# One pair of v columns computed plainly, with the mLSTM's gate columns in the same pass

## The chip, the cores and the metric

The kernel runs on one core of a Trainium2 chip. The core's engines run on their own instruction streams and meet through semaphores: TensorE (PE in the profile; PEld is its loading of the stationary operand), VectorE (DVE), ScalarE (ACT), GpSimd (POOL), and SyncE (SP), which issues nearly all DMAs. The metric is the device time of one execution in microseconds (us).

## The reference

One layer of an encoder on 1024 prompt and 256 sample tokens of width 2048, all float32. What matters here is its beginning, the normalization and the one combined projection, whose columns feed all later parts:

```python
hn = rmsnorm(x, norm_w)
proj = jnp.einsum('btd,dp->btp', hn, w_in)
cuts = [int(c) for c in np.cumsum([NA_WIDTH] * 4 + [2 * ML_WIDTH, ML_WIDTH, ML_WIDTH, ML_WIDTH])]
na_q, na_k, na_v, na_g, ml_qk, ml_v, ml_o, ml_z, ml_gp = jnp.split(proj, cuts, axis=-1)
...
gates = ml_gp.astype(f32).reshape(B, T, 2, 2, ML_HEADS) + gate_b.astype(f32)
h = bidirectional_mlstm(mq, mk, mv, gates)
```

The projection has 9 x 1024 columns and 16 gate columns. Queries, keys and values of the neighbourhood attention (8 heads of 128) come first, then its SiLU gate, then the mLSTM's q and k (which pass a convolution of width 5), v, o and z. The factors norm_w (by K) and 1/rms (by token) can be taken apart: the kernel multiplies x by norm_w beforehand, and the result of a projection by the token's 1/rms afterwards.

## The kernel before

**Number format.** Each float32 operand is split into a high and a low part that TensorE takes (hi is a rounded copy, made on ACT; lo = source - hi, made on DVE; functions split and split_a). A product is three matmuls: hi x hi, hi x lo, lo x hi.

**Stages.** The first stage (up to about 1095 us) projects the first 768 tokens; the second stage projects the other 512 tokens, and attention, mLSTM and the output projection follow and interleave. This change is in the first stage.

**A pair of the first stage** (pair_a). The 72 tiles of 128 columns are taken in pairs, named by the first tile's number: 0 to 7 q, 8 to 15 k, 16 to 23 the gate of the attention, 24 to 39 q and k of the mLSTM, 40 to 47 o, 48 to 55 z, 56 to 71 the values (256 columns a pair). A pair is a 2 x 2 x 2 block product (two column tiles, two halves of K = 2048, two halves of 384 tokens), done with seven products instead of eight, in the manner of Strassen and Winograd. The seven combinations of x are made once and stay in SBUF (xop(i, kk, b_) gives combination i, K tile kk, hi or lo). 1 is the first half of K of the first tokens and 2 the second half of K of the same tokens; 3 is the second half of K of the other tokens, and 7 that minus their first half of K. The combinations of weights are sums of 256 columns on POOL (summed, tiles named t), split into tiles named s. The weights are the stationary operand and 384 tokens the moving one: 7 products x 8 K tiles x 3 = 168 matmuls of 384 columns a pair. The seven PSUM banks are then added up on DVE (plus) and scaled by 1/rms (scaled), which gives the two tiles c with columns on the partitions and tokens along the free axis.

**What follows a pair** (finish_a) is a generator that the next pair drives on between its own products: splits and stores for q and k, the convolution for 24 to 38 (many DVE operations), tanh on ACT and a store for o and z. Values are wanted with tokens on the partitions, so a pair of v needs 12 transposes on PE (L475), after which they are copied as hi and lo into a tile vo and stored (store_v).

**The gates** (gates_a) run once, behind pair 6: weight sums on DVE, four tiles that POOL clears and that take the split weights, 64 matmuls of 384 tokens (L596), two copies, and six small products (L604) that bring the tokens to the partitions; DVE then scales by 1/rms and adds the bias into gt.

**The order of the pairs** is a list:

```python
order = [4, 6]
rest = list(range(KT0, QK0, 2)) + list(range(OT0, NCH, 2))
for i in range(NU):
    order += [QK0 + 2 * i, NCH + 2 * i, *rest[2 * i : 2 * i + 2]]
```

It gives 4, 6, 24, 56, 8, 10, 26, 58, 12, 14, ... (KT0 = 8, QK0 = 24, OT0 = 40, NCH = 56). Before some pairs, x_square loads a tile xq of the other tokens and squares it on ACT. Ten of the pairs (SECOND: 24, 8, 10 among them) also store four of their weight sums (sD) for the second stage.

**Buffers.** Weight tiles of 512 KB (named r) and the tiles xq share a ring of three (tag ra); splits of weights a ring of eight (wsa); results and what is made from them a ring of five (pc); vo has one buffer besides. PSUM has three banks under the tag pr and five under a. Who comes when on each engine, and which free buffer a tile gets, is settled by a scheduler with a model of its own when the program is built; the code's order gives the priorities.

**In the second stage** proj_v does what its name says with the tokens as the stationary operand and the weights as the moving one. Its first call takes the 16 gate columns along as columns 257 to 272 (tile pv, L774).

Of the kernel before, what the change touches and what calls it, by code (L numbers as in the profile page):

```python
# [14 lines left out]
P = 128  # L15
# [33 lines left out]
def kernel(  # L49
# [3 lines left out]
    xtok: bass.AP,  # L53
    w_in: bass.AP,
    w_g: bass.AP,
    w_o: bass.AP,
    lnw: bass.AP,
    rpb_tab: bass.AP,
# [14 lines left out]
    def f(ap):  # L73
        return ap.bitcast(F32)

    def bank(tag, name):
        return ps.tile([P, 512], F32, tag=tag, name=name, bufs=3 if tag == "pr" else 5)
# [106 lines left out]
    def split_a(hi, lo, src):  # L184
        S.copy(hi, src)  # L185
        last_split["ins"] = V.tensor_tensor(lo, src, f(hi), op=ALU.subtract).ins
# [102 lines left out]
    def pc(name):  # L289
        return wa.tile([P, GA], F32, tag="pc", name=name, bufs=NPC)  # L290

    def wsa(name):
        return wa.tile([P, 2, 256], F32R, tag="wsa", name=name, bufs=NWS)
# [145 lines left out]
    def finish_a(n1, Cn):  # L439
# [28 lines left out]
        if n1 >= NCH:  # L468
# [3 lines left out]
            for tt in range(GA // P):  # L472
# [8 lines left out]
                store_v((n1 - NCH) // 2, tt * P, vo, b[:, :256])  # L481
                yield

    def pair_a(n1, bg=iter(()), hook=None, first=False, pinned=False):
        nm = f"A{n1}"
        tags = ("pr", "pr", "pr", "a", "a", "a", "a")
# [82 lines left out]
            pass  # L569
        return finish_a(n1, Cn)  # L570

    def gates_a():
        raw = wa.tile([P, 1024], F32, tag="ra", name="gAw", bufs=NRA)
        DM.dma_start(raw[:, :256], w_g)
        ab = [raw[:, :P], raw[:, P : 2 * P]]
        ext = [raw[:, 256 : 256 + P], raw[:, 384 : 384 + P]]
        V.tensor_tensor(ext[0], ab[0], ab[1], op=ALU.add)
        V.tensor_scalar(ext[1], ab[0], -1.0, None, op0=ALU.mult)
        st = []
        for i, src in enumerate((*ab, *ext)):  # L580
            t = wsa(f"gAt{i}").rearrange("p h c -> p (h c)")[:, : 8 * 32 + 96]
            G.memset(f(t), 0.0)
            tv = t[:, :256].rearrange("p (k h c) -> p k h c", h=2, c=16)
            sv = src.rearrange("p (k c) -> p k c", c=16)
            split_a(tv[:, :, 0, :], tv[:, :, 1, :], sv)
            st.append(t)
        sel = raw[0:32, 512:528]
        V.tensor_tensor(sel, ident[0:32, 0:16], ident[0:32, 16:32], op=ALU.add)
        gs = pc("gAg")
        for th, prods in enumerate((((0, 1), (1, 2)), ((2, 3), (3, 7)))):  # L590
            b = bank("a", f"gAb{th}")[:, :HALF]
            n = 0
            for w_, i in prods:
                for kk in range(8):
                    for hl_ in range(2):
                        PE.matmul(  # L596
                            b, st[w_][:, kk * 32 : kk * 32 + P], xop(i, kk, hl_),
                            start=n == 0, stop=n == 31,
                        )
                        n += 1  # L600
            V.tensor_copy(gs[0:32, th * HALF : (th + 1) * HALF], b[0:32])
        for tt in range(GA // P):
            b = bank("a", f"gAt{tt}")
            PE.matmul(b[:, :16], gs[0:32, tt * P : (tt + 1) * P], sel, start=True, stop=True)  # L604
            V.scalar_tensor_tensor(
                gt[:, tt, :], b[:, :16], rcs[0][:, tt : tt + 1], gb_sb, op0=ALU.mult, op1=ALU.add
            )

    opening = first_tiles()
    next(opening)  # L610
    cw_sb = const.tile([P, 16, 5], F32, tag="cw", name="cw_sb")
# [6 lines left out]
    DM.dma_start(w4_sb, mlnw)  # L618
    V.tensor_scalar(w4_sb, w4_sb, 0.25, None, op0=ALU.mult)
    order = [4, 6]  # L620
    rest = list(range(KT0, QK0, 2)) + list(range(OT0, NCH, 2))
    for i in range(NU):
        order += [QK0 + 2 * i, NCH + 2 * i, *rest[2 * i : 2 * i + 2]]
    pools = []

    def second_pools():
# [3 lines left out]

    bg = opening
    for i, n1 in enumerate(order):
        bg = pair_a(n1, bg, second_pools if i == len(order) - 1 else None, i == 0, i == 1)
        if i == 1:
            gates_a()
        k = i - 4
        if 0 <= k < 8:
            x_square(1, k)
        if k == 8:
            x_rstd(1)  # L640
# [1135 lines left out]
def _layout(inputs):  # L1776
    import numpy as np

    g = {k: np.asarray(v) for k, v in inputs.items()}
    x = np.concatenate([g["x_prompt"][0], g["x_sample"][0]], axis=0)  # L1780
    xT = np.ascontiguousarray(x.reshape(TT, KT, P).transpose(2, 1, 0))
    w = g["w_in"][0]
    cols = {}
    o = 0
    for name, n in (("q", 1024), ("k", 1024), ("v", 1024), ("g", 1024), ("qk", 2048),
                    ("mv", 1024), ("mo", 1024), ("mz", 1024), ("gp", 16)):
        cols[name] = w[:, o : o + n]
        o += n
    ch = np.concatenate([cols[n] for n in ("q", "k", "g", "qk", "mo", "mz", "v", "mv")], axis=1)
    nb = NCH + 2 * NU  # L1790
    w_in = np.ascontiguousarray(
        ch.reshape(2, 4, 2, P, nb // 2, 2, P).transpose(4, 1, 3, 5, 0, 2, 6).reshape(nb // 2, 4, P, 1024)
    )
    gorder = [d * 8 + w_ * 4 + h for w_ in range(2) for d in range(2) for h in range(4)]
    w_g = np.ascontiguousarray(
        cols["gp"][:, gorder].reshape(KT, P, 16).transpose(1, 0, 2).reshape(P, KT * 16)
    )
    w_o = np.ascontiguousarray(
        g["w_out"][0].reshape(KT, P, 4, 512).transpose(2, 1, 0, 3).reshape(4, P, KT * 512)
    )  # L1800

    rpb = g["na_rpb"][0]
    i = np.arange(P)

    def table(qr, qc, kr, kc, rows):
        wr = min(8, rows)
        rs = np.clip(qr - wr // 2, 0, rows - wr)[:, None]
        cs = np.clip(qc - 8, 0, 48)[:, None]
        ok = (kr >= rs) & (kr < rs + wr) & (kc >= cs) & (kc < cs + 16)
        ro = np.clip(kr - qr[:, None] + 7, 0, 14)  # L1810
        co = np.clip(kc - qc[:, None] + 15, 0, 30)
        return np.where(ok[None], rpb[:, ro, co], np.float32(NEG))
# [11 lines left out]
    return {  # L1824
        "xT": xT,
        "xtok": np.ascontiguousarray(x),
        "w_in": w_in,
        "w_g": w_g,
        "w_o": w_o,
        "lnw": np.ascontiguousarray(g["ln_w"][0].reshape(KT, P).T),  # L1830
        "rpb_tab": tab,
        "conv_w": np.ascontiguousarray(g["ml_conv_w"][0].reshape(5, 16, P).transpose(2, 1, 0)),
        "conv_b": np.ascontiguousarray(g["ml_conv_b"][0].reshape(16, P).T),
        "gate_b": np.ascontiguousarray(g["ml_gate_b"][0].reshape(16)[gorder]),
        "mlnw": np.ascontiguousarray(g["ml_norm_w"][0].reshape(8, P).T),
        "fnw": np.ascontiguousarray(g["final_norm_w"]),
    }
# [24 lines left out]
```

## Time and profile before

| | us |
|---|---|
| median of 3 runs | 2547.41 |
| lowest and highest | 2546.06, 2548.14 |
| the profiled execution | 2548.95 |
| its span, from first to last instruction | 2547.2 |

The profiled execution is 1.54 us above the median. Its span is 1.75 us shorter than its time. TensorE's granted clock was 0.999 of full speed, in every slice of the page at 9 tenths or more.

How to read the rows: a group row gives line, engine, operation, the names of the tiles (out <- in, numbers left out), the shape and a count. A timeline row gives start and length in us; matmuls overlap, so what one costs is the distance of starts, not its length. In square brackets stands an idle time before a row, and who ended it. A window row gives the stretch, its length, then busy us and the number of instructions of PE, PEld, DVE, ACT and POOL, the granted clock, the DMA engines' share and GB/s. A row that ends in "to landing" gives the time from a DMA's issue to its landing.

### The profile page before, as it was taken

What the parts mean: (1) busy time and instruction counts of PE and PEld (TensorE: products, weight loads), DVE (VectorE), ACT (ScalarE), POOL (GpSimd) and SP (SyncE); (2) the same over time, 40 slices, a digit from 0 to 9 for tenths busy, and PEclk for the clock granted to TensorE, in tenths of its full rate; (3) what the DMA queues carried; (4) which work ended last, traced back from release to release, by engine and by line L of the source; (5) the groups of instructions that cost most, each with busy time, mean ns of one, the idle gap of its engine ahead of it and who ended that gap; (6) DMA issues with size and microseconds to landing.
All of it is one profiled execution on the core that took longest, in us unless ns stands there. A gap on an engine that the chain in (4) does not pass through costs nothing.

```text
span 2547.2 us, 44847 instructions
## 1 busy us (share of the span) xinstructions
PE 2530.2 (99%) x15165; PEld 2370.7 (93%) x15165; DVE 1979.9 (78%) x4050; ACT 1348.7 (53%) x3053; POOL 597.9 (23%) x895
## 2 busy tenths in 40 slices
PE   9999999999999999999999999999999999999998
PEld 9999999999999999999999899899998888888887
DVE  8868788898969798988875676776775665889696
ACT  8635545444444444465655665666665553344445
POOL 0535555444444444410000011010100103000002
PEclk9999999999999999999999999999999999999999
DMA  6556474536434343476778878888877849646227
GB/s 217 164 159 204 137 231 129 182 120 194 131 112 127 108 129 100 135 245 211 232 247 272 267 267 288 273 261 266 298 230 240 291 126 352 204 145 212 90 87 256
DMA packets 307757, 505.67 MB, mean 199 GB/s; under 512 B 48992, under 2 KB 195080, under 8 KB 307528
## 3 DMA queue, kind: packets, MB, share of 16 engines
q1 hardware_dynamic: 304424, 490.75, 60.0%
q0 software_dynamic: 2960, 11.80, 1.2%
q8 instruction: 120, 1.97, 0.3%
q14 instruction: 109, 0.89, 0.1%
q10 hardware_dynamic: 144, 0.26, 0.0%
HBM read 374.18 MB, written 128.52 MB: 197 GB/s over the span
## 4 chain that ended last, share of the span: by engine, by line
PE 84%; DMA 2%; DVE 1%; issue 0%; ACT 0%; SPq 0%; POOLq 0%; POOL 0%; ACTq 0%; DVEq 0%
PE pc L691 16%; PE po L1681 15%; PE pv L774 6%; PE A40b L287 1%; PE A16b L287 1%; PE A52b L287 1%; PE A48b L287 1%; PE A44b L287 1%; PE A20b L287 1%; PE A42b L287 1%; PE A22b L287 1%; PE A14b L287 1%; PE A38b L287 1%; PE A50b L287 1%; PE A68b L287 1%; PE A46b L287 1%
## 5 line engine op out<-in xcount | busy, mean ns | idle before, releaser
L1681 PE MATMUL po<-wo,mo 128*128 128x512 f32 (+1 forms) x1620 | 374.2, 392 | 0.0
L1681 PEld LDWEIGHTS po<-wo,mo 128*128 128x128 f32 x1620 | 303.5, 188 | 70.0
L179 DVE TENSOR_TENSOR ws<-wr,ws 128x512 fp32r<-128x512 f32 x144 | 98.5, 693 | 38.4 <-ACT ws L178 37.9
L178 ACT CAST ws<-wr 128x512 fp32r<-128x512 f32 x144 | 87.6, 617 | 65.7 <-PE pc L691 58.0
L178 ACT CAST mo<-mb 128x640 fp32r<-128x640 f32 x72 | 52.0, 727 | 110.0 <-PE po L1681 99.5
L119 POOL TENSOR_SCALAR rs<-rs 128x1 f32<-128x1 f32 x9 | 4.2, 468 | 370.0 <-DVE rs L1634 366.9
L179 DVE TENSOR_TENSOR mo<-mb,mo 128x640 fp32r<-128x640 f32 x72 | 58.9, 826 | 30.8 <-ACT mo L178 30.8
L1602 DVE TENSOR_TENSOR y<-y,po 128x512 f32<-128x512 f32 x89 | 57.3, 685 | 13.9 <-PE po L1681 13.7
L178 ACT CAST mo<-ms 128x640 fp32r<-128x640 f32 x40 | 28.9, 725 | 51.2 <-PE po L1681 30.8
L179 DVE TENSOR_TENSOR wsv<-wr_v,wsv 128x512 fp32r<-128x512 f32 x64 | 44.3, 698 | 13.2 <-ACT wsv L178 13.0
L178 ACT CAST wsv<-wr_v 128x512 fp32r<-128x512 f32 x64 | 38.9, 616 | 23.7 <-PE pv L774 12.6
L429 DVE SCALAR_TENSOR_TENSOR pcv<-pco,cw_sb,pcv 128x516 f32<-128x516 f32 x48 | 36.8, 767 | 7.0 <-ACT pcv L423 7.0
L179 DVE TENSOR_TENSOR mo<-ms,mo 128x640 fp32r<-128x640 f32 x40 | 32.9, 821 | 10.0 <-ACT mo L178 10.0
L1616 ACT ACTIVATE jk<-y 128x512 f32<-128x512 f32 x39 | 24.5, 629 | 27.1 <-DVE y L1602 26.8
L1115 POOL MEMSET mls_0v<- 128x2 f32 x4 | 0.4, 101 | 160.4 <-DVE S_dt.float L179 136.9
L132 ACT ACTIVATE xq<-xq 128x1024 f32<-128x1024 f32 x20 | 21.2, 1061 | 31.4 <-DMA xq<-in_xtok_dram 29.0
L287 PE MATMUL fb<-xg,fw 128*128 128x384 f32 x192 | 34.7, 335 | 0.1
L287 PEld LDWEIGHTS fb<-xg,fw 128*128 128x128 f32 x192 | 33.3, 188 | 0.4 <-ACT xg L185 0.4
L1565 DVE TENSOR_TENSOR ms<-mb,mb 128x640 f32<-128x640 f32 x40 | 32.8, 821 | 0.0
L264 DVE TENSOR_TENSOR pco<-pc,rstdb 128x512 f32<-128x512 f32 x28 | 19.1, 687 | 16.6 <-PE pc L691 15.7
L812 DVE CUSTOM_DVE_ANT_0 nap_0st<-nap_0s,nap_0bt 128x384 f32<-128x384 f32 x32 | 17.7, 553 | 15.7 <-PE nap_0s L807 7.8
L815 ACT ACTIVATE nap_0st<-nap_0st,nap_0sm 128x384 f32<-128x384 f32 x32 | 19.7, 617 | 19.0 <-DVE nap_0sm L812 19.0
(2790 smaller groups left out, 8524.1 us busy)
## 6 DMA issues: line engine op xcount, KB each, us to landing
wr<-in_w_in_dram SPq DMA_DIRECT2D x72, 512.0 KB, 4.9
wr_v<-in_w_in_dram SPq DMA_DIRECT2D x32, 512.0 KB, 5.5
wb<-in_w_o_dram SPq DMA_DIRECT2D x48, 256.0 KB, 3.9
xq<-in_xtok_dram SPq DMA_DIRECT2D x20, 512.0 KB, 5.0
mb<-mx POOLq DMA_DIRECT2D x32, 320.0 KB, 7.9
y<-in_xtok_dram SPq DMA_DIRECT2D x35, 256.0 KB, 5.1
wr_wp<-in_w_o_dram SPq DMA_DIRECT2D x16, 512.0 KB, 6.2
vS<-vo SPq DMA_DIRECT2D x24, 256.0 KB, 5.1
```

The source lines that it names most:

```text
L132: S.activation(raw, raw, AF.Square, accum_out=ssq[g][:, t, q : q + 1])
L178: S.copy(hi, src)
L179: return V.tensor_tensor(lo, src, f(hi), op=ALU.subtract)
L287: PE.matmul(o, w(a_), x(b_), start=first and m == 0, stop=last and m == 2)
L429: V.scalar_tensor_tensor(dst[:, a:n], src[:, a + j - pad : n + j - pad], cw_sb[:, ct, j : j + 1], dst[:, a:n], op0=ALU.mult, op1=ALU.add,)
L691: PE.matmul(pb[j], t[j][:, wi, c : c + P], xs[xi], start=first and m == 0, stop=last and m == 2,)
L774: PE.matmul(outs[tt], xs[:, tt * P : (tt + 1) * P], t[:, wi, q * w : (q + 1) * w], start=first and m == 0 and (gates or tt % 2 == 0), stop ...
L815: S.activation(st, st, AF.Exp, bias=sm[:, 0:1], scale=-1.0, accum_out=sm[:, 2:3])
L1565: V.tensor_tensor(t, x, y_, op=op)
L1602: V.tensor_tensor(Y[p, q, tt], Y[p, q, tt], bk, op=op)
L1616: S.activation(jk, Y[p, q, tt], AF.Square, accum_out=ss[t][:, c : c + 1])
L1681: PE.matmul(bk[tt] if o is None else o, m[xi][:, tt * P : (tt + 1) * P], w[wi][:, cs], start=first and kk == 0 and j == 0, stop=last and j ...
```

## The change

A new function unit_vg takes the place of the v pair 56 and of gates_a. It makes the 256 columns of the first v pair and the 16 gate columns as a plain product, without the seven-product scheme: the tokens are the stationary operand in six tiles of 128, the 272 columns are the moving one, and six PSUM banks (two halves z of three tiles tt) collect the sums over all of K in one pass. It uses combinations of x that are there: 1 and 2 for the first tokens, and for the other tokens (a + b) with 3 minus a with 7, where a and b are the weights of K's first and second half. Values and gates come out with tokens on the partitions, so the transposes of this pair go, and so do the folds; 1/rms is now applied in the copies out of PSUM. The split weights (vgs) lie in the ring pc, the weight tiles (vgr, 272 KB) in ra, and the copies (vgo) in vo and pc by turns. The list of pairs becomes 4, 6, 24, 8, 40, 56, 26, 58, 10, 12, ...: the unit stands at 56, two places later than the pair did, behind pair 40, and nothing is left to be finished behind it. The pairs 10 to 22 each move on to the next place that such a pair had; from 42 on the list is as before.

```diff
+    def unit_vg(bg):
+        banks = {(z, tt): bank("a" if z else "pr", f"vg{z}{tt}")[:, :272] for z in range(2) for tt in range(3)}
+        for kk in range(8):
+            raw = wa.tile([P, 1024], F32, tag="ra", name=f"vgr{kk}", bufs=NRA)
+            DM.dma_start(raw[:, :544], w_vg[kk])
+            a, b = raw[:, 0:272], raw[:, 272:544]
+            ab = raw[:, 544:816]
+            G.tensor_tensor(ab, a, b, op=ALU.add)
+            for i, z, src, scale in ((1, 0, a, None), (2, 0, b, None), (3, 1, ab, None), (7, 1, a, -1.0)):
+                t = wa.tile([P, GA], F32R, tag="pc", name=f"vgs{kk}{i}", bufs=NPC)
+                t = t[:, :544].rearrange("p (h c) -> p h c", h=2)
+                last_split["ins"] = split(t[:, 0], t[:, 1], src, scale).ins
+                for tt in range(3):
+                    for m, (xi, wi) in enumerate(((0, 0), (0, 1), (1, 0))):
+                        PE.matmul(
+                            banks[z, tt], xop(i, kk, xi)[:, tt * P : (tt + 1) * P], t[:, wi],
+                            start=kk == 0 and i in (1, 3) and m == 0,
+                            stop=kk == 7 and i in (2, 7) and m == 2,
+                        )
+                if i in (2, 7):
+                    next(bg, None)
+        for _ in bg:
+            pass
+        for z, tt in banks:
+            k = 3 * z + tt
+            rc = rcs[0][:, k : k + 1]
+            if k % 2:
+                vo = wa.tile([P, GA], F32R, tag="pc", name=f"vgo{k}", bufs=NPC)
+                vo = vo[:, :512].rearrange("p (a d) -> p a d", a=2)
+            else:
+                vo = wa.tile([P, 2, 256], F32R, tag="vo", name=f"vgo{k}", bufs=1)
+            store_v(0, k * P, vo, banks[z, tt][:, :256], rc)
+            V.scalar_tensor_tensor(
+                gt[:, k, :], banks[z, tt][:, 256:], rc, gb_sb, op0=ALU.mult, op1=ALU.add
+            )
+        return iter(())
...
-    def gates_a():
...
-    rest = list(range(KT0, QK0, 2)) + list(range(OT0, NCH, 2))
+    rest = [KT0, OT0, *range(KT0 + 2, QK0, 2), *range(OT0 + 2, NCH, 2)]
     for i in range(NU):
         order += [QK0 + 2 * i, NCH + 2 * i, *rest[2 * i : 2 * i + 2]]
+    order[3:6] = [KT0, OT0, NCH]
...
-        bg = pair_a(n1, bg, second_pools if i == len(order) - 1 else None, i == 0, i == 1)
-        if i == 1:
-            gates_a()
+        if n1 == NCH:
+            bg = unit_vg(bg)
+        else:
+            bg = pair_a(n1, bg, second_pools if i == len(order) - 1 else None, i == 0, i == 1)
...
+    wv = np.concatenate([cols["v"][:, :256], cols["gp"][:, gorder]], axis=1)
+    w_vg = np.ascontiguousarray(wv.reshape(2, 8, P, 272).transpose(1, 2, 0, 3).reshape(8, P, 544))
```

Where the gates stood, on PE, before: the gates' last products, the three first of the six small ones (gAt), and the start of pair 24. In a name such as A24b5, 24 is the pair and 5 the product; s is a split weight, and its last digit the product.

```order
L596 MATMUL gAb1_1785<-xg2_6_269,gAt3_1745 128x384 x2
L596 MATMUL gAb1_1785<-xg2_7_273,gAt3_1745 128x384 x2
L604 MATMUL gAt0_1819<-gAw_1729,gAg_1750 128x16
L604 MATMUL gAt1_1822<-gAw_1729,gAg_1750 128x16
L604 MATMUL gAt2_1825<-gAw_1729,gAg_1750 128x16
L287 MATMUL A24b1_1837<-xb0_242,A24s01_1846 128x384 x3
L287 MATMUL A24b1_1837<-xb1_246,A24s01_1846 128x384 x3
```

The same place now:

```order
L288 MATMUL A6b2_1381<-xg0_7_271,A6s32_1705 128x384 x3
L288 MATMUL A6b3_1382<-xg0_6_267,A6s33_1718 128x384 x3
L288 MATMUL A6b3_1382<-xg0_7_271,A6s33_1718 128x384 x3
L288 MATMUL A24b1_1729<-xb0_242,A24s01_1738 128x384 x3
L288 MATMUL A24b1_1729<-xb1_246,A24s01_1738 128x384 x3
L288 MATMUL A24b5_1730<-xg1_0_244,A24s05_1750 128x384 x3
```

Pair 24 follows the last product of pair 6 without anything between.

Ahead of pair 26, on ACT, before: behind pair 10, the square of a token tile, pair 10's last casts, and pair 26's first.

```order
L132 ACTIVATE xq1_1_3252,ssq1_232<-xq1_1_3252 128x1024
L185 CAST A10s31_3165<-A10r3_3163 128x256
L185 CAST A10s35_3178<-A10t35_3175 128x256
L185 CAST A10s36_3190<-A10t36_3187 128x256
L185 CAST A10s34_3200<-A10r3_3163 128x256
L185 CAST A10s37_3212<-A10t37_3209 128x256
L185 CAST A10s32_3227<-A10r3_3163 128x256
L185 CAST A10s33_3241<-A10t33_3238 128x256
L185 CAST A26s01_3264<-A26r0_3262 128x256
```

The same place now, behind the unit (vgs73 and vgs77 are the splits of its last two groups of nine matmuls):

```order
L133 ACTIVATE xq1_1_3221,ssq1_232<-xq1_1_3221 128x1024
L182 ACTIVATE vgs67_3122<-vgr6_3083 128x272
L179 CAST vgs71_3137<-vgr7_3134 128x272
L179 CAST vgs72_3149<-vgr7_3134 128x272
L186 CAST A26s01_3233<-A26r0_3231 128x256
L179 CAST vgs73_3161<-vgr7_3134 128x272
L186 CAST A26s05_3244<-A26t05_3242 128x256
L182 ACTIVATE vgs77_3173<-vgr7_3134 128x272
```

Two casts of pair 26 now stand among the last casts of the work ahead of it.

The start of pair 26 on PE, before:

```order
L287 MATMUL A26b1_3255<-xb0_242,A26s01_3264 128x384 x3
L287 MATMUL A26b1_3255<-xb1_246,A26s01_3264 128x384 x3
L287 MATMUL A26b5_3256<-xg1_0_244,A26s05_3275 128x384 x3
L287 MATMUL A26b5_3256<-xg1_1_248,A26s05_3275 128x384 x3
L287 MATMUL A26b4_3258<-xg2_0_245,A26s04_3303 128x384 x3
L287 MATMUL A26b4_3258<-xg2_1_249,A26s04_3303 128x384 x3
L287 MATMUL A26b7_3259<-xg2_0_245,A26s07_3322 128x384
L287 MATMUL A26b6_3257<-xg1_0_244,A26s06_3294 128x384 x3
```

And now, from its second product (b7) on:

```order
L288 MATMUL A26b7_3228<-xg2_0_245,A26s07_3275 128x384
L288 MATMUL A26b1_3224<-xb0_242,A26s01_3233 128x384 x3
L288 MATMUL A26b1_3224<-xb1_246,A26s01_3233 128x384 x3
L288 MATMUL A26b5_3225<-xg1_0_244,A26s05_3244 128x384 x3
L288 MATMUL A26b5_3225<-xg1_1_248,A26s05_3244 128x384 x3
L288 MATMUL A26b7_3228<-xg2_0_245,A26s07_3275 128x384 x2
L288 MATMUL A26b7_3228<-xg2_1_249,A26s07_3275 128x384 x3
L288 MATMUL A26b2_3229<-xg0_0_243,A26s02_3284 128x384 x3
L288 MATMUL A26b2_3229<-xg0_1_247,A26s02_3284 128x384 x3
L288 MATMUL A26b3_3230<-xg0_0_243,A26s03_3295 128x384
L288 MATMUL A26b6_3226<-xg1_0_244,A26s06_3255 128x384 x3
```

Products 4 and 7 now come first, and product 6, whose bank held the unit's third (vg02), comes last but for the rest of product 3.

More of the change, by code (lines that the diff above doesn't have):

```diff
@@ L55 @@
     w_g: bass.AP,
+    w_vg: bass.AP,
     w_o: bass.AP,
@@ L570, in pair_a @@
         return finish_a(n1, Cn)
-    def gates_a():
[L573 to L607, printed above, removed]
     opening = first_tiles()
@@ L1828, in _layout @@
         "w_g": w_g,
+        "w_vg": w_vg,
         "w_o": w_o,
```

## The prediction

> **What bounds the kernel now.** First the page's busy line and the chain that ended last, then the waits of TensorE in the first stage (74 to 1095 us), then TensorE's timeline at the places that the change touches.
>
> ```profile
> span 2547.2 us, 44847 instructions
> PE 2530.2 (99%) x15165; PEld 2370.7 (93%) x15165; DVE 1979.9 (78%) x4050; ACT 1348.7 (53%) x3053; POOL 597.9 (23%) x895
> ...
> PE 84%; DMA 2%; DVE 1%; issue 0%; ACT 0%; SPq 0%; POOLq 0%; POOL 0%; ACTq 0%; DVEq 0%
> ```
>
> TensorE (PE) is busy for 99% of the span and carries 84% of the chain. A busy PE need not be at its peak, so I look at what it waits for. These are all its waits between 74 and 1095 us: line, who is waited for, sum, times, longest.
>
> ```profile
> PE rsps L160 <- DVE rstdb L161: 0.6, 1, 0.6
> PE A4b L287 <- ACT A4s L185: 0.5, 1, 0.5
> PE A6b L287 <- DVE A4c L499: 0.4, 1, 0.4
> PE A12b L287 <- DVE A58c L499: 0.3, 1, 0.3
> PE A4b L287 <- DVE A4s L186: 0.3, 1, 0.3
> ```
>
> They sum to 2.1 us in 1021. The first stage is a row of matmuls without gaps, so its length is the number of matmuls times their spacing. What the change takes from that row it takes from the span, unless it opens a gap.
>
> **What goes.** PE's timeline, start and length in us, at the gates (L596, L604) and at the starts of pairs 24, 56, 8, 10 and 26:
>
> ```profile
> 131.11 6.40 PE L287 MATMUL A6b<-xg,A6s 128*128 128x384 f32 x36
> 137.35 2.95 PE L596 MATMUL gAb<-xb,gAt 128*128 128x384 f32 x16
> 140.13 8.52 PE L596 MATMUL gAb<-xg,gAt 128*128 128x384 f32 x48
> 148.58 0.84 PE L604 MATMUL gAt<-gAw,gAg 32*128 32x16 f32 x6
> 149.35 1.32 PE L287 MATMUL A24b<-xb,A24s 128*128 128x384 f32 x6
> ...
> 152.90 0.84 PE L604 MATMUL gAt<-gAw,gAg 32*128 32x16 f32 x6
> ...
> 179.84 1.20 PE L287 MATMUL A56b<-xb,A56s 128*128 128x384 f32 x6
> ...
> 208.97 1.20 PE L287 MATMUL A8b<-xb,A8s 128*128 128x384 f32 x6
> ...
> 239.42 1.20 PE L287 MATMUL A10b<-xb,A10s 128*128 128x384 f32 x6
> ...
> 268.77 1.20 PE L287 MATMUL A26b<-xb,A26s 128*128 128x384 f32 x6
> ```
>
> - Pair 56 itself: 208.97 - 179.84 = 29.13 us for 168 matmuls of 384 columns, 173.4 ns each. This is the length of an undisturbed pair.
> - The gates: 149.35 - 137.35 = 12.00 us, and what their second half adds to pair 24: (179.84 - 149.35) - 29.13 = 1.36 us. Together 13.36.
> - The 12 transposes of pair 56, which run inside pairs 8 and 10: (239.42 - 208.97) - 29.13 = 1.32 and (268.77 - 239.42) - 29.13 = 0.22. Together 1.54.
>
> The sum of what goes is 29.13 + 13.36 + 1.54 = 44.03 us of PE time.
>
> **What comes.** 288 matmuls of 272 columns (8 double tiles of K, 4 splits each, 3 token tiles, 3 passes). The second stage has that very shape already: v and gates for 512 tokens, 192 matmuls, whose stationary side is an x tile and whose moving side is 272 columns of split weights. First row and the row behind the last one, then the loads and matmuls of one x tile in that stretch (ns min/median/max):
>
> ```profile
> 1095.35 0.41 PE L774 MATMUL pv<-wsv,x_0h 128*128 128x272 f32 x2
> ...
> 1119.44 0.40 PE L774 MATMUL pv<-wsv,x_0h 128*128 128x256 f32 x2
> 1120.73 0.39 PE L774 MATMUL pv<-wsv,x_0h 128*128 128x256 f32 x1 [0.89 <-DVE wsv L179]
> ...
> L774 PEld LDWEIGHTS pv<-wsv,x_0h x9: 187/188/189, 1095.2 to 1119.3; 128*128 128x128 f32 x9
> L774 PE MATMUL pv<-wsv,x_0h x8: 284/286/288, 1095.4 to 1100.8; 128*128 128x272 f32 x8
> ```
>
> (1119.44 - 1095.35) / 192 = 125.5 ns each, so 288 take 36.14 us. The gain before any new wait is 44.03 - 36.14 = 7.89 us.
>
> Here a rule speaks against the change. The Trainium skill, "TensorE: Matmul & The Clock Gate", Part 3 (The mechanism), says that a weight load overlaps running matmuls only when it goes to another row group; all loads here fill the whole array. With that page's figures (a load 128/1.2 = 107 ns, a stream N/2.4 + 2.5 ns) a 272-column matmul would be 223 ns and a 384-column one 269 ns: 288 of the one are 64.1 us, 232 of the other 62.4 us (an estimate from that page), and 7.9 us of gain would shrink to about 1.4. The trace disagrees: a load is 188 ns long and the matmuls follow each other at 125.5.
>
> **New waits and moved steps**, each against what covers it. Busy us of PE, PEld, DVE, ACT, POOL in the gates' stretch, in pair 56 and in the second stage's unit:
>
> ```profile
> 137.35:149.35 12.00, 12.00 (x72) 11.72 (x71) 7.93 (x19) 3.69 (x9) 2.41 (x4) 1.00 0.51 150
> 179.84:208.97 29.13, 29.13 (x170) 29.13 (x170) 28.84 (x46) 15.21 (x35) 15.07 (x15) 1.00 0.41 118
> 1095.35:1119.44 24.09, 24.09 (x194) 24.07 (x193) 20.59 (x42) 16.62 (x32) 4.45 (x13) 1.00 0.67 225
> ```
>
> - Pair 24 now follows pair 6 at once, so VectorE (DVE) loses 12 us of cover, in which it folded pair 6. It now starts in the order of products in which pair 26 started behind pair 10, at 268.77, without a wait. DVE was busy 7.93 us in the gates' stretch, over 1 us of it the gates' own. I take 0; bound 0 to 2.
> - Pair 8 instead of 56 now hosts the convolution of pair 24, with DVE at 28.84 of 29.13 us and no PE wait. Pair 8 also stores its sums, 16 more DMAs on SP, whose buffers POOL waits for. I take 0; bound 0 to 0.6, the stage's longest wait.
> - Work that moves or shrinks off the path: 12 stores of v (two places later), pair 8's key and sum stores and pair 40's two stores (earlier), on SP; 8 sums and no memsets on POOL instead of 16 and 4; on DVE eleven folds and scalings of some 0.5 us fewer, six small gate sums more. Nothing in this stage reads v or gates. 0, since PE covers it.
> - Into the unit: its split weights sit in a ring of five buffers (pc) that also holds pair 40's two results until they are stored. Pair 40 as it ran before (its results' store, its landing, PE's next pair):
>
> ```profile
> L466 SPq DMA_DIRECT2D pT<-A40c x2: 319/320/320, 717.4 to 718.4; - x2
> ...
> DMA to landing us min/median/max: 2.5/2.5/2.5
> ...
> 712.04 1.20 PE L287 MATMUL A42b<-xb,A42s 128*128 128x384 f32 x6
> ```
>
> The two buffers come free 717.4 + 2.5 - 712.04 = 7.9 and 8.9 us after pair 40's last matmul. A group of nine matmuls is 1.13 us, and the unit asks for these two for its 10th and 12th group, at 10.2 and 12.4 us. Until then three buffers carry it: use, release, cast and subtract are some 2.2 us, three groups are 3.4. I take 0; bound 0 to 0.9, the wait at 1120.73, where a unit of this kind met the next.
> - Out of the unit: the hi and lo copies of every second bank use one buffer (vo), so the third bank's copy waits for the first one's store. On ACT that copy stands ahead of four casts of pair 26, and PE needs the bank for pair 26's 32nd matmul. Copies and store of pair 56, and all such stores:
>
> ```profile
> L178 ACT CAST A56vo<-A56v x6: 366/372/372, 219.3 to 243.8; 128x256 fp32r<-128x256 f32 x6
> L179 DVE TENSOR_TENSOR A56vo<-A56v,A56vo x6: 410/416/426, 222.2 to 244.2; 128x256 fp32r<-128x256 f32 x6
> ...
> vS<-vo SPq DMA_DIRECT2D x16, 128.0 KB, 3.8
> ```
>
> The first bank's copies end about when the unit does. Two issues and 3.8 us of landing bring 4.5 us; hi, lo and gates of the third bank 0.37 + 0.42 + 0.23 more, 5.6 us with the hand-over from engine to engine. PE arrives after 31 x 0.1734 = 5.4 us. I take 0.4 us; bound 0 to 2.
>
> The sum: 2548.95 (the profiled execution) - 7.89 + 0.4 = 2541.5. That execution is 1.54 us above the median of the runs, 2547.41, so against the median I forecast 2539.9 us, 0.3% faster. 0.2%, 5.1 us, is about what a measurement of this kernel can tell from no change.
>
> **The rivals.**
>
> Late loads before the unit's last casts. On ACT the first cast of pair 26 stands ahead of the casts of the unit's last two groups. It needs tile A26r0, loaded into the buffer of a token tile (xq) that must first be loaded and squared. Landing of such loads, and the work on them:
>
> ```profile
> L132 ACT ACTIVATE xq<-xq x8: 1059/1061/1066, 223.8 to 429.0; 128x1024 f32<-128x1024 f32 x8
> ...
> DMA to landing us min/median/max: 3.7/3.8/5.2
> ...
> L185 ACT CAST A58s<-A58r x12: 388/406/407, 290.8 to 317.9; 128x256 fp32r<-128x256 f32 x12
> L186 DVE TENSOR_TENSOR A58s<-A58r,A58s x12: 410/419/960, 291.2 to 322.3; 128x256 fp32r<-128x256 f32 x12
> ...
> DMA to landing us min/median/max: 3.8/3.9/3.9
> ...
> mb<-mx POOLq DMA_DIRECT2D x32, 320.0 KB, 7.9
> ```
>
> From the unit's start: the buffer for the token tile is free after the 19th of 32 groups and one cast and subtract, 21.5 + 0.9; load 3.8, square with its read-out 1.25, load 3.9, cast, the next cast and subtract 1.25: 32.6 us. PE needs that group's weights at 30 x 1.13 = 33.9 us. The margin is 1.3 us, which speaks against this rival; that both loads run through one queue with the ring's own loads speaks for it. If each took 7.9 us, the page's longest median, PE would wait 8.1 - 1.3 = 6.8 us: 2546.7 us, still not slower. Chance 0.13, anywhere from 2542 to 2547.
>
> The gates were cover. If all of DVE's work in the gates' stretch that is not the gates' own, some 6 us, came to lie before pair 24's matmuls, the change would shorten less than it says: 2546 us. Against it: in pair 56's row DVE is at 99% and PE has no gap. Chance 0.09, from 2541.5 to 2546.
>
> Slower, the weight load sets the spacing. If the loads of the unit's stationary x slices did not overlap, each matmul would take at least a load's 188 ns: 288 x 188 = 54.1 us, 18.0 more than above, and the kernel would take 2557.9 us. It decides from 44.03 / 288 = 152.9 ns per matmul on. For it: 288 loads for 78336 streamed columns, against 168 for 64512 in a pair. Against it: the second stage's 125.5 ns at the same shape, and 173.4 ns in a pair, also under 188. It is the rule of the Trainium skill named above, and the one case I find that ends on the other side. Chance 0.05.
>
> That the change doesn't do what it says is the second rival in another form: the matmuls are fewer by count, so only a new gap can keep the time.
>
> **How the numbers follow.** Forecast as summed, 0.73, with 2538.3 (no new wait at all, and 1.2 us of scatter) to 2542.3. Late loads 0.13, lost cover 0.09, weight loads 0.05. The range is 2538.3 to 2545: outside lie the slower case (0.05), the upper halves of the two middle ones (0.10), and a little below. Faster by over 0.2%, below 2542.3: 0.73 and a few hundredths of the middle cases, 0.76. Within 0.2%: 0.19. Slower: 0.05.
>
> **What would show it.** In the profile after: the unit's 288 matmuls (vg) from first to last in 36.1 us; pair 24 starting at once behind pair 6, and 29.1 us long; pair 26 with one wait of under 1 us, for DVE on the third bank; no wait of PE on ACT inside the unit's last two groups. The forecast is wrong if the unit is longer than 38 us, if pair 24 or pair 8 is over 30 us, or if gaps appear in pairs that the change only moved.

## The result, and the profile after

The changed kernel takes 2541.71 us (median of 11 runs, 2538.65 to 2544.98), the kernel before on the same chip 2547.64 us (11 runs, 2546.06 to 2550.17). The ratio is 0.9975 with a 95% interval of 0.9967 to 0.9982: faster, by 5.9 us. The forecast was 2539.9 us, 1.8 us too low.

The profiled execution took 2541.71 us too, its span is 2540.0 us. From its page, the span, the busy line and the chain:

```profile
span 2540.0 us, 44864 instructions
PE 2523.1 (99%) x15197; PEld 2363.7 (93%) x15197; DVE 1980.9 (78%) x4034; ACT 1348.3 (53%) x3052; POOL 597.7 (24%) x883
...
PE 87%; DMA 2%; DVE 2%; issue 0%; ACT 0%; POOL 0%; SPq 0%; POOLq 0%; ACTq 0%; DVEq 0%
```

PE is busy for 7.1 us less than before, and the span is 7.2 us shorter. So the time went where it was looked for, in PE's row of matmuls. PE's timeline at the starts of pairs 6, 24, 8 and 40, of the unit (vg), of pairs 26 and 58, and of the second stage:

```profile
106.68 1.20 PE L288 MATMUL A6b<-xg,A6s 128*128 128x384 f32 x6
...
136.68 1.20 PE L288 MATMUL A24b<-xb,A24s 128*128 128x384 f32 x6
...
165.81 1.20 PE L288 MATMUL A8b<-xb,A8s 128*128 128x384 f32 x6
...
194.94 1.20 PE L288 MATMUL A40b<-xb,A40s 128*128 128x384 f32 x6
...
224.54 0.92 PE L499 MATMUL vg<-vgs,xb 128*128 128x272 f32 x6
...
260.65 1.38 PE L288 MATMUL A26b<-xg,A26s 128*128 128x384 f32 x7
263.80 1.29 PE L288 MATMUL A26b<-xb,A26s 128*128 128x384 f32 x6 [1.77 <-DVE gt L517]
264.92 5.37 PE L288 MATMUL A26b<-xg,A26s 128*128 128x384 f32 x29
270.13 1.20 PE L288 MATMUL A26b<-xb,A26s 128*128 128x384 f32 x6
...
291.98 1.20 PE L288 MATMUL A58b<-xb,A58s 128*128 128x384 f32 x6
...
1088.82 0.41 PE L777 MATMUL pv<-wsv,x_0h 128*128 128x272 f32 x2
```

Pairs 24 and 8 are 29.13 us long, the unit is 36.11 us. Two places are not as forecast. Pair 26 takes 31.33 us, 2.20 more than an undisturbed pair, and after its seventh matmul PE waits 1.77 us for DVE. (The list counts a wait from the modelled end of the matmul before it. By the starts, 263.80 is 1.94 us later than 260.65 + 7 x 0.1734.) Pair 40 takes 29.60 us, 0.47 more, with a wait of 0.2 us for DVE that it did not have before. PE's waits between 74 and 1095 us, the first and last of five:

```profile
PE A26b L288 <- DVE gt L517: 1.8, 1, 1.8
...
PE A40b L288 <- DVE A40s L187: 0.2, 1, 0.2
```

The balance of the two profiled executions (2548.95 - 2541.71 = 7.24 us) is then as follows. From pair 6's first matmul to the second stage's, 987.85 us became 982.14: 5.71 us, about the forecast 7.89 less pair 26's 2.20. That the two agree so closely is in part luck: pair 40's 0.47 us came on top, and the pair that hosts the transposes of pair 58 became 0.62 us shorter (31.06 us for pair 12 before, 30.44 for pair 10 now), which nobody forecast. The other 1.5 us lie where the change touches nothing: 0.82 in the opening (pair 6 starts at 107.50 before and 106.68 after) and 0.67 behind the first stage (1451.85 to 1451.18). The start of pair 6 lies between 105.8 and 107.5 us in the profiled executions of this study, so the opening's share is scatter. What lies behind the first stage varies between 1449.6 and 1453.7 us in them.

What DVE did just before it came to the unit's banks (vgo is the copy, gt the scaled gates), and what POOL did then:

```profile
256.73 0.98 DVE L180 TENSOR_TENSOR vgs<-vgr,vgs 128x272 fp32r<-128x272 f32 x1
257.63 0.95 DVE L187 TENSOR_TENSOR A26s<-A26t,A26s 128x256 fp32r<-128x256 f32 x1
258.50 0.98 DVE L183 SCALAR_TENSOR_TENSOR vgs<-vgr,vgs 128x272 fp32r<-128x272 f32 x1
...
260.29 0.41 DVE L187 TENSOR_TENSOR A26s<-A26r,A26s 128x256 fp32r<-128x256 f32 x1
...
263.04 0.47 DVE L183 SCALAR_TENSOR_TENSOR vgo<-vg,rstdc,vgo 128x256 fp32r<-128x256 f32 x1
263.43 0.22 DVE L517 SCALAR_TENSOR_TENSOR gt<-vg,rstdc,gb_sb 128x16 f32<-128x16 f32 x1
```
```profile
255.78 0.74 POOL L574 TENSOR_TENSOR A26t<-A26r 128x256 f32<-128x256 f32 x1 [9.63 <-DMA A26r<-in_w_in_dram]
...
259.15 0.93 POOL L574 TENSOR_TENSOR A26t<-A26r 128x256 f32<-128x256 f32 x1
260.51 0.79 POOL L574 TENSOR_TENSOR A26t<-A26t,A26r 128x256 f32<-128x256 f32 x1 [0.43 <-DVE A26s L187]
```

The load of pair 26's first weight tile landed at 255.7 us. Until then POOL, ACT and DVE had nothing to do for it; then its sums and splits came all at once, in the last 5 us of the unit. Six splits on DVE that started while POOL was at a sum (four of pair 26, two of the unit) took 0.94 to 0.98 us; those that started while POOL stood still took 0.41, and one fell in between (0.63, at 256.18). DVE was busy without a break from 256.18 us on, and the copies stood behind these splits in its order. So it reached the first bank's copy at 263.04 us, though ACT had made its half of it by 260.3 us.

A smaller loss is too short for the list. The 29 matmuls from 264.92 us on take 5.21 us, 0.18 more than 29 x 0.1734. It falls on pair 26's 32nd matmul, at 268.1 us, the first that needs the third bank: DVE was done with that bank at 268.06 us, since its copy had to wait for the first bank's store (ACT started it at 266.92, after 5.53 us of waiting for that store).

### The profile page after: what moved, and what is told of

Read it like the earlier page. It is cut to its first block, busy times and chain, and to the rows that moved or that the text cites. A ratio compares the mean times of both kernels' runs of the same rounds, so it can differ in the third digit from the quotient of the medians.

```text
span 2540.0 us, 44864 instructions
## 1 busy us (share of the span) xinstructions
PE 2523.1 (99%) x15197; PEld 2363.7 (93%) x15197; DVE 1980.9 (78%) x4034; ACT 1348.3 (53%) x3052; POOL 597.7 (24%) x883
## 4 chain that ended last, share of the span: by engine, by line
PE 87%; DMA 2%; DVE 2%; issue 0%; ACT 0%; POOL 0%; SPq 0%; POOLq 0%; ACTq 0%; DVEq 0%
PE pc L694 16%; PE po L1684 15%; PE pv L777 5%; PE A22b L288 1%; PE A44b L288 1%; PE A14b L288 1%; PE A18b L288 1%; PE A10b L288 1%; PE A48b L288 1%; PE A52b L288 1%; PE A50b L288 1%; PE A42b L288 1%; PE A20b L288 1%; PE A16b L288 1%; PE A12b L288 1%; PE A70b L288 1%
```

## The experiments

Of each kernel stand here the time (the median where there are several runs, and then the ratio to the kernel before with its 95% interval) and what its trace shows. The differences at the unit's exit are near the scatter of the runs; there the trace decides.

**What the gain is made of.** First the kernel before with only the new list of pairs:

```diff
-    rest = list(range(KT0, QK0, 2)) + list(range(OT0, NCH, 2))
+    rest = [KT0, OT0, *range(KT0 + 2, QK0, 2), *range(OT0 + 2, NCH, 2)]
...
+    order[3:6] = [KT0, OT0, NCH]
```

> Edit to the kernel before: only the new order of the pairs (4, 6, 24, 8, 40, 56, 26, ...); pair 56 stays a seven-product pair, gates_a stays behind pair 6. Theory: the order costs and brings nothing that counts, since PE has hardly a wait in this stage with either: within 1.5 us of before. Rival (the place brings the gain): 2 us or more faster. Rival (hosting the convolution in pair 8, which also stores sums): up to 0.6 us of waits more.

2548.81 us, ratio 1.0003 (0.9994 to 1.0012). PE's waits in the first stage are four, of 0.6 us at most. The order by itself is worth nothing either way, and pair 8 hosts the convolution without a wait (29.1 us). Pair 40 behind it has the same wait of 0.2 us and the same length (29.63 us) as in the changed kernel: that loss comes with the order and not with the unit.

Then the kernel before without its gates:

```diff
         if i == 1:
-            gates_a()
+            G.memset(gt[:, : GA // P], 0.0)
```

> Edit to the kernel before: gates_a is left out, gt is cleared instead (the mLSTM then gets gates of zero for these tokens). Theory: the gates cost the 13.36 us that PE's timeline shows: 2534.3 us, -13.4 against before. Rival (the gates were cover for DVE, which folds pair 6 in that time): pair 24 gets waits or becomes longer than 29.1 us, and the gain is 2 to 6 us less: 2536 to 2540 us.

2532.81 us, ratio 0.9942 (0.9930 to 0.9955), which is 11.5 to 17.8 us. The forecast -13.4 lies in it. The trace is closer. Pair 24's start and pair 56's:

```profile
135.68 1.20 PE L287 MATMUL A24b<-xb,A24s 128*128 128x384 f32 x6
...
164.81 1.20 PE L287 MATMUL A56b<-xb,A56s 128*128 128x384 f32 x6
```

Pair 24 is 29.13 us long with the gates gone, and no wait stands there. DVE did not need the gates' 12 us as cover, and that rival falls.

Then the changed kernel with 256 columns in the unit, and gates_a back behind pair 6:

```diff
-        banks = {(z, tt): bank("a" if z else "pr", f"vg{z}{tt}")[:, :272] for z in range(2) for tt in range(3)}
+        banks = {(z, tt): bank("a" if z else "pr", f"vg{z}{tt}")[:, :256] for z in range(2) for tt in range(3)}
...
+        if i == 1:
+            gates_a()
```

> Edit to the kernel after: the unit makes the 256 v columns alone, and gates_a is back behind pair 6. Theory: a plain pair costs more than a seven-product pair with its transposes: 288 matmuls at 125.5 - 16 x 0.43 = 118.6 ns are 34.2 us, against 29.13 + 1.54 = 30.67; with the exit's 1.8 us that is 5.3 us more than before: 2552 to 2553 us. So the gain of the whole change comes from the gates alone, which cost 13.36 us apart and 2 us as columns. Rival (the plain form is itself the gain, since it saves transposes, folds and DVE time): at or below before.

2553.41 us, ratio 1.0022 (1.0013 to 1.0031): slower than before, by 5.4 us. The unit's first row, and the exit:

```profile
237.51 0.86 PE L499 MATMUL vg<-vgs,xb 128*128 128x256 f32 x6
...
272.00 1.33 PE L288 MATMUL A26b<-xg,A26s 128*128 128x384 f32 x6
273.97 1.31 PE L288 MATMUL A26b<-xb,A26s 128*128 128x384 f32 x6 [0.65 <-DVE vgo L183]
...
280.06 1.66 PE L288 MATMUL A26b<-xg,A26s 128*128 128x384 f32 x8 [0.93 <-DVE vgo L183]
```

(272.00 - 237.51) / 288 = 119.8 ns a matmul, 34.5 us, against 34.2 expected. A plain pair of v is 3.8 us dearer than the seven-product pair with its transposes (30.67), and its exit cost another 1.6 us of waits (pair 26 is 31.40 us long, 2.3 too much). The whole gain is the gates: apart they take 13.4 us, as 16 more columns 36.11 - 34.49 = 1.6. The parts add up: 13.4 - 1.6 - 3.8 and 2.2 for the exit leave 5.8 us, against 5.9 measured.

**Does the weight load set the spacing?** Every matmul of the unit was cut in two, so that each x slice is loaded twice:

```diff
-                        PE.matmul(
-                            banks[z, tt], xop(i, kk, xi)[:, tt * P : (tt + 1) * P], t[:, wi],
+                        for c in (0, 136):
+                            PE.matmul(
+                                banks[z, tt][:, c : c + 136], xop(i, kk, xi)[:, tt * P : (tt + 1) * P],
+                                t[:, wi, c : c + 136],
```

> Edit: each of the unit's 288 matmuls of 272 columns becomes two of 136 columns with the same stationary slice: 576 loads for the same columns. If the streamed columns alone set the spacing (as the prediction took it; 125.5 ns at 272 and 173.4 ns at 384 columns differ by 0.43 ns a column, and 8.8 ns are left per matmul), a matmul takes 67 ns and the unit 38.7 us: about 2544 us. If a full load sets a floor, the nearest rows are the 128-column transposes of the attention, three in 0.32 us, 107 ns each: the unit takes 61 us and the kernel about 2567 us. If loads need the 125.5 ns at which they follow each other now, the unit takes 72 us: 2578 us. The second is the likeliest: the load is near, but below, the stream at 272 columns. That would leave the prediction's sum right and its rival (load sets the spacing) wrong at 272 columns, true at narrower ones.

2566.45 us, ratio 1.0073 (1.0059 to 1.0087). The unit's first row, pair 26's first, and the unit's loads (ns min/median/max):

```profile
224.77 0.45 PE L500 MATMUL vg<-vgs,xb 128*128 128x136 f32 x3
...
289.04 1.25 PE L288 MATMUL A26b<-xb,A26s 128*128 128x384 f32 x6
...
L500 PEld LDWEIGHTS vg<-vgs,xg x432: 192/192/192, 226.0 to 288.9; 128*128 128x128 f32 x144
```

(289.04 - 224.77) / 576 = 111.6 ns. The unit takes 64.3 us; 61 had been expected for a floor. At half the columns the spacing hardly falls below the 125.5 ns of 272 columns, so a floor of some 112 ns shows. That the load sets it, and not the columns, is borne out by small products in the kernel before. Eight matmuls of 16 columns, each with a full load, start 101 ns apart (the next row starts at 1179.22 us):

```profile
1178.41 0.96 PE L988 MATMUL mgstri<-mgstmp,tris 128*128 128x16 f32 x8
```

Eight of 8 columns whose loads have 8 rows instead of 128 (L1021, from 1146.44 to 1147.00 us) start 70 ns apart, so a matmul with a small load takes well under 112 ns. So a full load sets the spacing at 136 columns, but not at 272. The unit keeps 14 ns off that floor, and the floor is 41 ns below the 152.9 ns from which on the slower rival would have come true. A load's own row of 192 ns is not its price, since the rows of successive loads overlap. The Trainium skill, "TensorE: Matmul & The Clock Gate", gives 128/1.2 = 107 ns for a load (LDWEIGHTS), which is 4% from the floor; its rule in Part 3 (The mechanism), that loads overlap matmuls only in another row group, would make 107 and 59 ns follow each other, 166 ns, and the trace disagrees at both widths.

**The wait at the unit's exit.** Four suspects: the late load, the contention of DVE with POOL, the single buffer vo, and the place of the copies in DVE's order. First the load. A26r's buffer comes from the ring of three in which a token tile xq was loaded and squared during the unit. This version loads none there:

```diff
-        k = i - 4
-        if 0 <= k < 8:
+        k = i - 4 - (i > 5)
+        if 0 <= k < 8 and i != 5:
             x_square(1, k)
```

> Edit: no token tile xq is loaded and squared while the unit runs; the ones that followed come one pair later each. Theory (late load): the 1.8 us wait at the start of pair 26 comes about because tile A26r0 waits for that token tile's buffer and lands at 255.74 us, 31.2 us after the unit's start; its sums and splits then fill DVE until 263.04, and the copies out of the unit's banks come after them. Without the token tile A26r0 should land some 4 to 5 us earlier (before 252), DVE's first bank copy should start by 261.5, and PE's wait should fall below 0.5 us; the time about 2540 us (1.3 to 1.8 less than after). Rival (one vo buffer, as the prediction had it): a wait of 0.4 to 1 us stays, on the third bank, since the store's 4 us are not touched. Rival (order on DVE): the copies stand behind eight splits of pair 26 in any case, and over 1 us of wait stays.

2538.74 us, ratio 0.9961 (0.9947 to 0.9975). PE has four entries in the list of waits of the first stage, none of them in the unit or pair 26. The first cast of pair 26 on ACT, DVE's first bank copy, and PE at the exit and at the start of pair 58:

```profile
250.65 0.41 ACT L186 CAST A26s<-A26r 128x256 fp32r<-128x256 f32 x1 [0.61 <-DMA A26r<-in_w_in_dram]
```
```profile
258.47 0.47 DVE L183 SCALAR_TENSOR_TENSOR vgo<-vg,rstdc,vgo 128x256 fp32r<-128x256 f32 x1
```
```profile
260.69 1.38 PE L288 MATMUL A26b<-xg,A26s 128*128 128x384 f32 x7
261.91 1.20 PE L288 MATMUL A26b<-xb,A26s 128*128 128x384 f32 x6
...
289.83 1.20 PE L288 MATMUL A58b<-xb,A58s 128*128 128x384 f32 x6
```

The tile lands 5 us earlier, DVE starts the copies 4.6 us earlier, and pair 26 has no wait and is 29.1 us long. Both rivals fall: vo still has its one buffer, and the copies still stand behind eight splits of pair 26. The version with the loads doubled agrees: there the unit is 28 us longer, the tile lands 16.5 us before the unit's end (4.9 in the changed kernel), and PE has no wait at the exit either.

The buffer by itself, with all six copies in the ring pc:

```diff
-            if k % 2:
-                vo = wa.tile([P, GA], F32R, tag="pc", name=f"vgo{k}", bufs=NPC)
-                vo = vo[:, :512].rearrange("p (a d) -> p a d", a=2)
-            else:
-                vo = wa.tile([P, 2, 256], F32R, tag="vo", name=f"vgo{k}", bufs=1)
+            vo = wa.tile([P, GA], F32R, tag="pc", name=f"vgo{k}", bufs=NPC)
+            vo = vo[:, :512].rearrange("p (a d) -> p a d", a=2)
```

> Edit: all six bank copies of the unit (vgo) take buffers of the ring of five (pc); the one-buffer tile vo is no longer used by the unit. Late load theory: ACT's idle time of 5.5 us before the third copy goes, but PE's wait on the first bank stays at 1.5 to 2 us, since DVE reaches the copies no earlier. Rival (one vo buffer): PE's wait goes or falls below 0.5 us.

One run, 2541.11 us. The wait is still there, on the first bank, since DVE reaches it at 262.97 us:

```profile
263.73 1.28 PE L288 MATMUL A26b<-xb,A26s 128*128 128x384 f32 x6 [1.52 <-DVE gt L514]
```

What goes is the small loss on the third bank: from 264.85 us on the 29 matmuls take 5.07 us, 0.04 more than 29 x 0.1734. So the single buffer costs 0.1 to 0.2 us here, and no part of the wait on the first bank.

Then the contention, with the late load kept and the four sums of pair 26's first tile left out:

```diff
             def summed(i, x, y_, op):
+                if n1 == 26 and r == 0:
+                    return x
```

> Edit: the four weight sums of pair 26's first double tile are left out (so its products 5, 6, 7 and 3 take an unsummed tile there); POOL is idle while DVE splits that tile, the load is as late as before. Theory that POOL slows DVE: between 256 and 263 us five DVE splits of pair 26 and two of the unit take 0.94 to 0.98 us while POOL makes sums, others 0.41 us. Without the sums all take about 0.41 us, DVE is done 3 to 4 us earlier, and PE's wait of 1.8 us goes to 0. The Trainium skill, SBUF - State Buffer, section Who interferes with whom, says that a DVE instruction with two SBUF inputs contends with a GpSimd instruction that reads SBUF; by it the same. Rival (the late load alone): the splits keep their length, DVE reaches the copies at 262 us or later, and over 1 us of wait stays.

One run, 2541.35 us; the wait is gone. DVE and POOL in the same stretch, and PE at the start of pair 58:

```profile
256.42 0.42 DVE L187 TENSOR_TENSOR A26s<-A26r,A26s 128x256 fp32r<-128x256 f32 x1 [1.97 <-ACT A26s L186]
256.76 0.43 DVE L180 TENSOR_TENSOR vgs<-vgr,vgs 128x272 fp32r<-128x272 f32 x1
...
260.23 0.97 DVE L183 SCALAR_TENSOR_TENSOR vgs<-vgr,vgs 128x272 fp32r<-128x272 f32 x1
261.12 0.95 DVE L187 TENSOR_TENSOR A26s<-A26r,A26s 128x256 fp32r<-128x256 f32 x1
261.99 0.47 DVE L183 SCALAR_TENSOR_TENSOR vgo<-vg,rstdc,vgo 128x256 fp32r<-128x256 f32 x1
```
```profile
258.10 1.04 POOL L576 TENSOR_TENSOR A26t<-A26r 128x256 f32<-128x256 f32 x1 [11.36 <-DMA A26r<-in_w_in_dram]
...
260.86 0.93 POOL L576 TENSOR_TENSOR A26t<-A26r,A26t 128x256 f32<-128x256 f32 x1
```
```profile
290.76 1.20 PE L288 MATMUL A58b<-xb,A58s 128*128 128x384 f32 x6
```

With POOL idle the same DVE instructions take 0.42 us, and as soon as POOL comes to the next tile's sums, from 258.10 on, 0.95 again. So that POOL slows DVE's splits is shown. DVE gained less than the 3 to 4 us expected, because the next tile's sums took the place of those left out. The unit starts at 225.24 us here, 0.7 us later than in the changed kernel, so the times have to be counted from there: the tile lands after 30.7 us (31.2 in the changed kernel), DVE reaches the first copy after 36.75 us (38.50), and pair 58 starts after 65.52 us (67.44, and 65.17 with the early load). So 1.9 of the 2.3 us go with these four sums, at a load that is only 0.5 us earlier. The late load and POOL's sums are both needed for the wait: with the early load the splits beside POOL's sums still take 0.97 us (at 251.64 us, for one), and nothing waits. In this build three matmuls of pair 26 stand ahead of the unit's last six on PE, and those six start 0.2 us late, when the low part of their weights is done at 261.20 us; that is most of the 0.35 us left.

The Trainium skill, "SBUF — State Buffer", section Who interferes with whom, says that a DVE instruction with two SBUF inputs contends with a GpSimd instruction that reads SBUF, and one with at most one such input, outside the two-port modes, does not. The trace agrees on both: in the version with the later token tiles a bank copy, which takes one tensor from PSUM and only one from SBUF, lasts 0.47 us at 258.47, while POOL is at a sum:

```profile
258.21 0.93 POOL L574 TENSOR_TENSOR A26t<-A26r 128x256 f32<-128x256 f32 x1
```

**The place.** The unit where pair 56 stood, directly behind pair 24, in the old order of the other pairs:

```diff
-    rest = [KT0, OT0, *range(KT0 + 2, QK0, 2), *range(OT0 + 2, NCH, 2)]
+    rest = list(range(KT0, QK0, 2)) + list(range(OT0, NCH, 2))
...
-    order[3:6] = [KT0, OT0, NCH]
```

> Edit to the kernel after: the unit stands where pair 56 stood, directly behind pair 24, in the old order of the other pairs; it then hosts the convolution of pair 24 on DVE, besides its own 32 splits. Theory (the place matters through the ring pc): the unit's split weights need the ring of five that the convolution also uses, so PE waits inside the unit, 2 us or more in all: 2544 us or more. Rival (the place doesn't matter): the unit takes 36.1 us as before and the time is 2540 to 2543 us.

2548.78 us, ratio 1.0004 (0.9995 to 1.0013): the whole gain is gone. PE's waits inside the unit (the first of three rows, 5.9 us in all), the unit as a window row, and ACT at the first and longest wait:

```profile
PE vg L499 <- ACT vgs L179: 3.4, 3, 2.6
```
```profile
165.59:211.73 46.14, 40.11 (x290) 37.90 (x289) 34.44 (x61) 20.59 (x47) 10.77 (x13) 0.96 0.36 106
```
```profile
169.20 1.02 ACT L424 ACTIVATE A24cv<-A24c,cb_sb,cw_sb 128x766 f32<-128x766 f32 x1 [8.53 <-DVE A24c L265]
170.13 0.40 ACT L179 CAST vgs<-vgr 128x272 fp32r<-128x272 f32 x1
```

The unit takes 46.1 us, 10 more than in its new place. That it gets slower was expected, but the ring pc is not what the longest wait shows: ACT stands for 8.5 us at the convolution's first instruction until DVE has folded and scaled pair 24, and the unit's casts are queued behind it. What the ring adds to the smaller waits was not taken apart. So the order is worth nothing to the kernel before, and 7 us to the unit.

**Once more, side by side.** The changed kernel and the version with the later token tiles, unchanged, on one chip:

> The changed kernel once more, on the same chip and against the same runs of before as the version with the later token tiles. Theory: 0.25% below before as measured at first, with the wait of 1.5 to 1.8 us at the start of pair 26. Rival (the forecast's smaller gain was scatter): the wait is not there again.

2541.44 us, ratio 0.9971 (0.9960 to 0.9982); the wait is there again:

```profile
PE A26b L288 <- DVE gt L517: 1.4, 1, 1.4
```

> The changed kernel with the token tiles moved one pair later, once more. Theory: the only thing that it saves is the wait at the start of pair 26, so it is 1.3 to 1.8 us faster than the changed kernel. Rival (it saves more, since the first runs put it 3.0 us ahead): 2.5 us or more. With some 1 us of scatter from run to run the trace decides: pair 26 of 29.1 us here, 30.9 to 31.3 there, and the other pairs equal.

2539.90 us, ratio 0.9962 (0.9949 to 0.9976). It is 1.5 us ahead by the medians; pair 26 takes 29.1 us against 31.3, and the other pairs behind pair 4 agree within 0.11 us. The two profiled executions are equally long even so (2538.7 us): from pair 6 to the second stage it is 980.06 us against 982.12, but behind the first stage 1451.85 against 1449.55, where the two versions are the same code and the executions vary by as much. Of the 3.0 us between their first medians about half was scatter. This is the best version found: 0.38% below the kernel before, about 1.5 to 2 us below the changed kernel, by the trace more surely than by the runs.

## Why the prediction was right, and where it was off

The forecast faster was right, in the predicted range, by the mechanism that it named. Point by point:

- **What goes, 44.03 us.** Right. The gates' 13.36 us are confirmed by the kernel without them (from pair 6's start to pair 24's it is 149.35 - 107.50 = 41.85 us in the kernel before and 29.9 there, and pair 24 is 1.36 us shorter), pair 56's 29.13 by the pairs that are left.
- **What comes, 36.14 us.** Right: 36.11, taken from the same shape in the second stage. The weight load sets the spacing only at smaller widths, at 112 ns (shown at 136 columns). One sum beside it is off: the gain by the figures of the Trainium skill, put at about 1.4 us, comes to some 2.1, namely 62.4 - 64.1 and the 3.8 us of what goes that are not the 232 matmuls (44.03 - 232 x 0.1734). Nothing rests on it.
- **Pair 24's lost cover 0, pair 8 as host 0, into the unit 0.** Right: 29.13 and 29.13 us, no wait of PE inside the unit. But by one of the prediction's own signs of being wrong, a gap in a pair that only moved, it missed something: pair 40, now behind pair 8, lost 0.47 us, and no step priced it. The unit at the old place shows what the entry would have cost with a convolution to host.
- **Out of the unit, 0.4 us for the single buffer vo on the third bank.** This is the step that failed, in size and in cause. The exit cost 2.2 us of pair 26's length, nearly all of it by a wait of 1.8 us on the first bank. What the step describes, the third bank behind the store, is there as well, but takes 0.15 us. The buffer caused no part of the wait on the first bank: with the load early no wait is left although vo is single, and with vo out of the way the wait stays. The step took it that "the first bank's copies end about when the unit does", with no queue ahead of them on DVE. It priced the copies (0.42 us; 0.47 measured) and left out the ten splits ahead of them. A row of such splits, 410/419/960 ns, stood at the rival of late loads, and there its median was taken; six of the ten took about the maximum. The bound of 2 us held for the listed wait, but not for the 2.2 us of pair 26.
- **The rival of late loads.** Its chain was timed almost exactly: A26r landed 31.2 us after the unit's start, by the rival's terms 21.5 + 0.9 + 3.8 + 1.25 + 3.9 = 31.35. But its consequence was sought in the unit's last casts alone. There it just did not come to a wait: the last split's low part was done at 259.48 us, and PE came to the last nine matmuls at 259.5. The same late tile then came out at the place of the other step, where the two were not put together.
- **The total.** Against the profiled execution 2541.5 was forecast, and 2541.71 came. That agreement flatters: the exit cost 1.8 us more, and 1.5 us of scatter in the opening and behind the stage gave most of it back. Against the medians, where such scatter averages out, the forecast is 1.8 us too low, the size of the failed term (1.6 if the sum starts from the kernel before's median of 11 runs, 2547.64). With the early load from pair 6 to the second stage 7.4 and 7.8 us are gained in its two profiled executions, close to the 7.89 that the prediction had before any new wait.

## What to carry to other kernels

When a new piece of work frees its banks through an engine that also prepares the next piece, add up that engine's queue at the hand-over in its order, with the durations that hold beside the other engines' work of that moment, and not with the medians. A load that arrives late costs at the place where its followers bunch up, which need not be the place that reads it. Columns that ride along as moving data in a product that must be made anyway cost little (1.6 us here for 16 columns), where a small product of its own cost 13.4.

## What the runs showed that was not expected

At the old place, PE's wait of 2.6 us was followed by a lower granted clock. Windows of that kernel, from the wait on (the clock is the third number from the end):

```profile
168.00:170.60 2.60, 0.02 (x1) 0.02 (x1) 1.51 (x4) 1.40 (x3) 0.00 (x0) 1.00 0.06 2
...
172.00:174.00 2.00, 2.00 (x10) 2.00 (x10) 1.96 (x3) 0.42 (x1) 0.00 (x0) 0.50 0.48 126
...
175.00:176.50 1.50, 1.23 (x11) 1.01 (x10) 0.59 (x2) 1.20 (x3) 0.89 (x1) 1.00 0.00 0
```

In 172 to 174 us ten matmuls ran at half the clock where sixteen would have, at 125.5 ns. By the starts, thirteen matmuls from 171.68 to 174.70 us took 3.02 us instead of 1.63, so 1.4 us were lost. The changed kernel's wait of 1.77 us had no such sequel; the 3.2 us behind it:

```profile
263.80:267.00 3.20, 3.20 (x18) 3.20 (x19) 1.45 (x6) 0.08 (x1) 0.00 (x0) 1.00 0.84 275
```
In the kernel with only the new order PE waits 2.16 us for a DMA at 1570.2 us, in the second stage, and the clock stays at 1.00 there too. So a wait of 2.6 us cost more than its length here; whether its length decides that, or where it fell, these three cases don't tell.
